# Three more weight tiles ahead of the branch, and the branch, the entry and the last two experts of each expert stage rearranged

## The chip, the cores and the metric

The kernel runs on one core of one Trainium2 chip. The metric is the device time of one execution in microseconds (us); for the kernel before it is the median of three runs. A core has five engines that run side by side, each with its own queue of instructions: TensorE (PE, matmuls), VectorE (DVE), ScalarE (ACT), GpSimd (POOL) and SyncE (SP, whose queue issues the transfers from memory here).

## The reference

Two layers over 256 tokens of width 1024. Layer 0 mixes the tokens by a convolution module, layer 1 by retention; behind each stands a mixture of 32 experts (top 2 of one group of 8). All weights are float32.

```python
for i in range(DEPTH):                      # 2 layers
    if i % 2 == 0: mix = conformer_conv(x, ...)
    else:          mix = retention(x, positions, ...)
    x = layer_norm(DEEPNORM_ALPHA * x + mix, ln1_g[i], ln1_b[i])
    ffn = hier_moe(x, ...)
    x = layer_norm(DEEPNORM_ALPHA * x + ffn, ln2_g[i], ln2_b[i])

def hier_moe(x, w_grp, b_grp, w_route, b_route, w_gate, w_up, w_down):
    ...  # combine: (256, 32), the two chosen experts' gates of each token, 0 elsewhere
    for e in range(N_EXPERTS):              # 32
        h = jax.nn.silu(xt @ w_gate[e]) * (xt @ w_up[e])     # 1024 -> 512, twice
        y = y + combine[:, e:e + 1] * (h @ w_down[e])        # 512 -> 1024
```

## The kernel before

**Stages.** Four stages follow one another: the convolution (0 to some 126 us), the experts of layer 0, the retention, the experts of layer 1. The text calls (e, q) the quarter q of the work of expert e.

**Weights.** The class `Weights` streams all weights through one queue, SP's, as pieces of 1 MiB, in the order in which they are used. An expert has six: gate and up by halves (two pieces each), down by halves (two). Each piece needs a tile: 12 ring tiles, in an expert stage two "own" ones more (pool `mp`) and two "split" ones (two half tiles each, `hi` and `lo`). `home(i)` says which kind piece i gets, `room` counts the free tiles, and `used()` gives a tile back and loads the next piece. So 16 pieces of a stage can be loaded before its first experts have used any. The pieces w12 to w27 are those of layer 0.

**The way in.** `norms` ends the stage before: for each half of the tokens (tt) it computes a layer norm, and `front(tt)` from `moe_front` transposes the result (tiles xr) and computes the router's logits (lg). Behind that, `moe` splits the activations into x1h and a remainder x1l (L898 on ScalarE, L899 on GpSimd), and `route` chooses the experts in small VectorE steps (`first_max`, L926 to L934; between them `warm` matmuls, which compute nothing that is used). TensorE counts positions (L953 to L955), and `gather` (L1011) collects up to 64 tokens for each expert by one-hot matmuls.

**An expert.** `gate_up` multiplies two 128-row slices of gate and up a quarter (L1025), `hidden` applies silu and the product, `turn` transposes h (L1045) and gathers the gates of a pair (L1049), `down` multiplies a pair of experts side by side in two column halves of the array (L1070), `places` and `parts` prepare the way back (L1080, L1090), and `scatter` adds a pair's result to the tokens (L1101). A table, `plan`, says behind which quarter of which expert each such step stands, a pair's steps one to two experts after its `gate_up`. The last pair (experts 30 and 31) stands outside the pattern: its 32 down matmuls come behind all gate and up, then `begin(1)` (L1110), then the scatter into PSUM, from which the norm at the end reads.

**The branch.** More than 64 tokens at one expert are handled by a loop in a branch (`extra`, L1126, `overflow`), which isn't entered with these inputs. All engines read the flag (L1128) and compare (L1134) at the same point of the program, between (0, 1) and (0, 2). The branch's scratch is in split tiles, and the tiles of the first two pieces are given back behind it:

```python
                if e == 0 and i == 1:
                    extra()
                    W.used(2)
                    for tt in range(2):
                        G.tensor_scalar(cur[:, tt], cur[:, tt], ALPHA, None, op0=OP.mult)
```

**Order.** `manual_schedule` keeps TensorE, ScalarE, VectorE and GpSimd in the order in which the code is written; SP's order is set by a scheduler. An instruction waits at the head of its engine's queue until what it needs is there, and all behind it wait with it.

## Time and profile before

| | us |
|---|---|
| median of three runs | 1322.53 |
| the three runs | 1321.91 to 1324.62 |
| the profiled execution | 1325.74 |
| its span | 1324.0 |
| mean granted TensorE clock | 0.977 of full |
| TensorE busy | 1264.8 (96%) |
| moved by DMA | 459.44 MB, mean 347 GB/s |

The profile is one execution, seen by the chip's profiler. The span is its time from the first to the last instruction. Busy time is time in which an engine executes; matmuls overlap one another, so the distance of two starts says more of what a matmul costs than its duration. An idle time is put down to the event that came last before the next instruction. The DMA share is the mean busy share of the core's 16 DMA engines. The clock stands as a share of full speed: 1.00 is 2.4 GHz, 0.50 is 1.2 GHz.

### The profile page before, as it was taken

How to read it: one execution, taken by the hardware profiler on the slowest of the kernel's cores; microseconds unless marked ns; L12 is line 12 of the kernel's file. 1: busy time of each engine (PE TensorE's matmuls, PEld its weight loads, DVE VectorE, ACT ScalarE, POOL GpSimd, SP SyncE). 2: the span in 40 equal slices, each digit the busy share in tenths (PEclk: the TensorE clock that was granted, in tenths of full speed). 3: DMA queues.
4: the chain of work that ended last, by engine and by line, in shares of the span. 5: the costliest groups of instructions: out<-in, count | busy, mean ns of one | idle time of the engine just before them, and what ended most of it. 6: DMA issues, size and time to landing. Idle time of an engine off the chain costs nothing. (4 is left out here: it accounts for less than half of the span.)

```text
span 1324.0 us, 15498 instructions
## 1 busy us (share of the span) xinstructions
PE 1264.8 (96%) x6139; PEld 668.2 (50%) x6139; DVE 491.0 (37%) x849; ACT 327.7 (25%) x543; POOL 164.0 (12%) x173
## 2 busy tenths in 40 slices
...
GB/s 299 399 110 185 98 387 418 426 425 425 426 425 427 425 426 425 426 426 408 247 173 202 175 193 210 100 369 419 425 425 426 425 426 426 425 425 426 425 428 125
DMA packets 102101, 459.44 MB, mean 347 GB/s; under 512 B 8226, under 2 KB 25410, under 8 KB 59010
## 3 DMA queue, kind: packets, MB, share of 16 engines
...
## 5 line engine op out<-in xcount | busy, mean ns | idle before, releaser
L1070 PE MATMUL y<-w,h 128*64 128x512 f32 x992 | 255.7, 595 | 14.8 <-DMA w<-in_moe_w_down_dram 14.8
L1025 PE MATMUL gu<-w,xghi 128*64 128x512 f32 x896 | 225.0, 612 | 0.0
L1036 DVE TENSOR_TENSOR h<-gl,gu 64x512 f32<-64x512 f32 x64 | 67.8, 1060 | 384.3 <-ACT gl L1034 372.4
L1025 PE MATMUL gu<-w,xglo 128*64 128x512 f32 x800 | 195.0, 612 | 6.6 <-PEq L1134 6.6
L1070 PEld LDWEIGHTS y<-w,h 128*64 128x64 f32 x992 | 78.1, 138 | 168.4 <-issue 143.2
L1025 PEld LDWEIGHTS gu<-w,xghi 128*64 128x64 f32 x896 | 62.4, 138 | 96.4 <-issue 88.4
L1025 PEld LDWEIGHTS gu<-w,xglo 128*64 128x64 f32 x800 | 55.8, 140 | 103.5 <-issue 97.0
L129 DVE TENSOR_TENSOR l<-w,h 128x1024 fp32r<-128x1024 f32 x64 | 81.2, 1270 | 67.9 <-ACT h L128 66.4
L1034 ACT ACTIVATE gl<-gu 64x512 f32<-64x512 f32 x64 | 37.6, 588 | 242.9 <-PE gu L1025 242.9
L128 ACT ACTIVATE h<-w 128x1024 fp32r<-128x1024 f32 x72 | 75.7, 1058 | 88.0 <-PE vg L763 31.7
L1052 ACT ACTIVATE h<-hT 128x256 f32<-128x256 f32 x64 | 24.6, 384 | 276.8 <-PE hT L1049 168.5
L1057 DVE COPY gsl<-hT 64x1 f32<-64x1 f32 x64 | 10.0, 156 | 188.1 <-ACT h L1052 187.7
L1105 DVE TENSOR_TENSOR cur<-sc,cur 128x512 f32<-128x512 f32 x116 | 72.3, 684 | 19.6 <-PE sc L1101 19.6
L129 POOL TENSOR_TENSOR l<-w,h 128x1024 fp32r<-128x1024 f32 x8 | 20.5, 2590 | 409.9 <-ACT h L128 409.9
L1090 ACT ACTIVATE yh<-y,gsl 128x512 fp32r<-128x512 f32 x64 | 44.0, 687 | 92.9 <-PE y L1070 90.5
L439 PE MATMUL pw<-xT,w 128*128 128x256 f32 x256 | 60.7, 394 | 1.8 <-DMA w<-in_conv_w_pw_dram 1.8
L472 POOL TENSOR_TENSOR gp<-gp,gt 128x256 f32<-128x256 f32 x76 | 56.2, 740 | 25.2 <-ACT gt L471 19.8
L1011 PE MATMUL gp<-oh,x1h 128*128 128x256 f32 x256 | 57.1, 304 | 2.3 <-DVE route L964 2.3
L1011 PEld LDWEIGHTS gp<-oh,x1h 128*128 128x128 f32 x256 | 38.6, 188 | 39.1 <-issue 38.1
L439 PEld LDWEIGHTS pw<-xT,w 128*128 128x128 f32 x256 | 50.3, 198 | 9.9 <-issue 2.7
L1083 DVE TENSOR_SCALAR s<-sp,cc 128x256 fp32r<-128x256 f32 x32 | 15.5, 484 | 96.3 <-PE sp L1080 96.3
L1011 PE MATMUL gp<-oh,x1l 128*128 128x256 f32 x256 | 50.8, 280 | 0.0
...
## 6 DMA issues: line engine op xcount, KB each, us to landing
w<-in_moe_w_down_dram SPq DMA_DIRECT2D x124, 1024.0 KB, 17.1
w<-in_moe_w_gate_dram SPq DMA_DIRECT2D x106, 1024.0 KB, 15.5
w<-in_moe_w_up_dram SPq DMA_DIRECT2D x106, 1024.0 KB, 16.2
w<-in_ret_w_qkvg_dram SPq DMA_DIRECT2D x24, 1024.0 KB, 13.2
...
w<-in_ret_w_o_dram SPq DMA_DIRECT2D x8, 1024.0 KB, 4.9
w<-in_conv_w_pw_dram SPq DMA_DIRECT2D x4, 1024.0 KB, 11.2
...
```

The lines of the kernel that those rows point to most:

```text
L128: self.nc.scalar.activation(hi, w, AF.Copy)
L129: (self.nc.gpsimd if pool else self.nc.vector).tensor_tensor(lo, w, hi.bitcast(F32), op=OP.subtract)
L439: PE.matmul(ps[:, 1 - g], w[g][:, kt], xT[:, kt], start=kt == 0, stop=kt == KT - 1)
L472: G.tensor_tensor(gps[c], gps[c], t, op=OP.add)
L1011: PE.matmul(ps[:, k], src[:, tt, q * 2 + k], o[:, tt].rearrange("p e c -> p (e c)"), start=i == 0, stop=i == 3)
L1025: PE.matmul(gus[e][m * CAP:(m + 1) * CAP], l, w[i % 2 * 2 + k], start=kt == 0, stop=kt == KT - 1)
L1034: S.activation(gl, gu[:CAP], AF.Silu)
L1036: V.tensor_tensor(hs[e].rearrange("s k p -> s p k"), gl.rearrange("s (p k) -> s p k", k=4), gu[CAP:].rearrange("s (p k) -> s p k", k=4), o ...
L1052: S.activation(hs[e], p, AF.Copy)
L1070: PE.matmul(ys[pr][n][j * CAP:(j + 1) * CAP], hs[e][:, kt], wds[e][kt % 2][:, n * 512:(n + 1) * 512], start=kt == 0, stop=kt == 3)
L1090: S.activation(yh[:, n], ys[pr][n], AF.Copy, scale=g)
L1105: V.tensor_tensor(o, ps, o, op=OP.add)
```

## The change

- **Tiles.** `ONCE` names three pieces of a stage (numbers 7, 16 and 17) that get tiles of their own, once: one a pair of split half tiles, two others four half tiles of the pool `hand`, which the transposed rows xr leave (`more`, called behind the norm). With them 19 pieces (w12 to w30) come before the branch, and the sequence of the other homes skips them.
- **Branch.** It stands behind (0, 3) instead of (0, 1); its scratch is in two ring tiles (`spare`). The scaling of `cur` behind it goes from GpSimd to ScalarE.
- **Entry.** The norm of the stage before is now called inside `moe`. The split x1h, x1l is done by quarters: ScalarE copies half the tokens in `front(tt)` (`high`), GpSimd takes one quarter of the remainder, VectorE three (`low`). `WARM` has two values less by one, and the last `first_max` has no warm matmuls at its end.
- **Last two experts.** Each goes alone: its down matmuls put the two halves of the output in the two column halves, its scatter uses 64 rows a half. Expert 30's first down steps move ahead of the end of expert 31's gate and up, `begin(1)` ahead of them, and the splits of the next stage's weights (`ahead`) stand among them: two by VectorE, two by GpSimd, where GpSimd had all four.
- The rotary tables are built at experts 3 and 10 instead of 0 and 4.

```diff
 RING = 12
+ONCE = {7: "split", 16: "hand", 17: "hand"}
 T4 = 9
 SPLIT = 4
-AH = 2
 ROWS_AT = (29, 0)
-WARM = [11, 8, 8, 0, 2, 0, 2, 3]
+WARM = [11, 8, 8, 0, 2, 0, 1, 2]
 YB = 2
...
     def home(self, i):
         for a, b in self.layers:
             if a <= i < b:
-                return ("ring", "own", "split")[max(0, (i - a) % (RING + 4) - RING + 2) // 2]
-        return "ring"
+                k = i - a
+                if k in ONCE:
+                    return "once", ONCE[k]
+                k -= sum(x < k for x in ONCE)
+                return ("ring", "own", "split")[max(0, k % (RING + 4) - RING + 2) // 2], None
+        return "ring", None
 
     def open(self, pool):
 
         self.own = pool
-        self.room.update(own=2, split=2)
-        self.load(4)
+        self.room.update(own=2, split=2, once=1)
+        self.load(6)
+
+    def more(self):
+
+        self.room["once"] = len(ONCE) - 1
+        self.load(2)
...
+    def spare(self, name):
+
+        t = self.ringp.tile([P, 2048], F32, tag="ring", name=name, bufs=RING)
+        return t[:, 0:1024], t[:, 1024:2048]
...
-    for p in range(NE // 2):
+
+    for p in range(NE // 2 - 1):
         e, both = 2 * p + 2, (2 * p, 2 * p + 1)
         planned(e - 1, 0, ("turn", e - 2))
-        if p < NE // 2 - 1:
-            planned(e, 0, ("turn", e - 1))
-            planned(e, 2, ("down", both, 0))
-            planned(e, 3, ("down", both, 1))
-            planned(e + 1, 0, ("down", both, 2))
-            planned(e + 1, 1, ("down", both, 3), ("parts", p))
+        planned(e, 0, ("turn", e - 1))
+        planned(e, 2, ("down", both, 0))
+        planned(e, 3, ("down", both, 1))
+        planned(e + 1, 0, ("down", both, 2))
+        planned(e + 1, 1, ("down", both, 3), ("parts", p), *([("place", -2)] if p == NE // 2 - 2 else []))
+        if p < NE // 2 - 2:
             planned(e + 2, 0, ("scatter", p))
-        else:
-            planned(e, 0, ("turn", e - 1), *[("down", both, k) for k in range(4)])
-    planned(NE - 2, 3, ("begin", 0))
+    z = NE - 1
+    planned(z - 1, 3, ("begin", 0))
+    planned(z, 0, ("turn", z - 1))
+    planned(z, 2, ("down", (z - 1,), 0), ("scatter", NE // 2 - 2), ("down", (z - 1,), 1), ("place", -1))
+    planned(z, 3, ("begin", 1), ("down", (z - 1,), 2), ("down", (z - 1,), 3), ("part", -2), ("turn", z),
+            *[("down", (z,), k) for k in range(4)], ("ahead", 2), ("part", -1), ("ahead", 4), ("scatter", -2),
+            ("scatter", -1))
...
+        def view(t, tt, n):
+            return t[:, tt, :, n * 64:(n + 1) * 64].rearrange("t k p -> t p k")
+
+        def row(tt, n):
+            return cur[:, tt, n * 512:(n + 1) * 512].rearrange("t (p k) -> t p k", k=KT)
+
+        def high(tt):
+            for n in range(2):
+                S.activation(view(x1h, tt, n), row(tt, n), AF.Copy)
+
+        def low(tt, n, eng=V):
+            eng.tensor_tensor(view(x1l, tt, n), row(tt, n), view(x1h, tt, n).bitcast(F32), op=OP.subtract)
+
         def front(tt):
             if tt == 0:
                 xT.extend(hand(f"xr{L}{q}", F32) for q in range(2))
                 mark["lg"] = sm1("lg")[:, 0:72].rearrange("p (a b) -> p a b", a=2)
+            else:
+                low(0, 1)
             lgp = mark["lg"]
             PE.matmul(lgp[:, tt], onesf[0:1, :], brt[0:1, L], start=True, stop=False, skip_group_check=True)
             transposes(tt, evac)
+            high(tt)
             ts = slice(tt * P, (tt + 1) * P)
             for kt in range(KT):
                 PE.matmul(lgp[:, tt], xT[kt // 4][:, kt % 4, ts], wrt[:, L, kt], start=False, stop=kt == KT - 1,
                           skip_group_check=True)
+            if not tt:
+                low(0, 0, G)
+            else:
+                low(1, 0)
+                mark["low"] = lambda: low(1, 1)
...
             W.open(mp)
             with tc.tile_pool(name=f"exp{L}", bufs=1) as ep:
-                for tt in range(2):
-                    v = cur[:, tt].rearrange("t (p k) -> t p k", k=KT)
-                    hv = x1h[:, tt].rearrange("t k p -> t p k")
-                    lv = x1l[:, tt].rearrange("t k p -> t p k")
-                    S.activation(hv, v, AF.Copy)
-                    G.tensor_tensor(lv, v, hv.bitcast(F32), op=OP.subtract)
-                route(L, ep, lgp, comb, posm, posT, flag)
+                norms(*prev, moe_front(L, x1h, x1l))
+                W.more()
+                route(L, ep, mark["lg"], comb, posm, posT, flag)
...
-            warm(WARM[7], f)
+            if not last:
+                warm(WARM[7], f)
...
-        m2, oh2 = first_max(me, 32)
+        m2, oh2 = first_max(me, 32, last=True)
...
+        mark["low"]()
...
+            single = e >= NE - 2
+            if single:
+                for j in range(2):
+                    for tt in range(2):
+                        PE.matmul(ps[j * CAP:(j + 1) * CAP, 256:257], ohs[e // 4][:, tt, e % 4].bitcast(F32),
+                                  comb[:, tt, e:e + 1], start=tt == 0, stop=tt == 1)
...
-                    j = e % 2
-                    PE.matmul(ys[pr][n][j * CAP:(j + 1) * CAP], hs[e][:, kt], wds[e][kt % 2][:, n * 512:(n + 1) * 512],
+                    j, b = (e % 2, n) if len(es) > 1 else (n, 0)
+                    PE.matmul(ys[pr][b][j * CAP:(j + 1) * CAP], hs[e][:, kt], wds[e][kt % 2][:, n * 512:(n + 1) * 512],
                               start=kt == 0, stop=kt == 3)
...
+                    ks = slice(0, P) if pr >= 0 else slice(n * CAP, (n + 1) * CAP)
                     for i in range(2):
-                        PE.matmul(ps, s0[pr][:, tt * P:(tt + 1) * P], ys[pr][i][:, n], start=not held and i == 0,
-                                  stop=i == 1 and (pr == NE // 2 - 1 or not held))
+                        PE.matmul(ps, s0[pr][ks, tt * P:(tt + 1) * P], ys[pr][i][ks, n if pr >= 0 else 0],
+                                  start=not held and i == 0, stop=i == 1 and (pr == -1 or not held))
...
+                elif what == "ahead":
+                    W.stop = len(pieces)
+                    W.ahead(*step, pool=step[0] > 2)
...
-            wts, big = [splitp.tile([P, 1024], F32, tag=t, name=f"ov{t}{L}") for t in ("hi", "lo")]
-            mid = [ep.tile([P, 512], F32, tag="gl", name="ovgl")[:CAP]]
-            mid += [hand(n, F32).rearrange("p a t -> p (a t)")[:CAP] for n in ("ovh", "ovy")]
+            (wts, big), mid = [W.spare(f"ov{n}{L}") for n in range(2)]
+            mid = [ep.tile([P, 512], F32, tag="gl", name="ovgl")[:CAP], *[m[:CAP] for m in mid]]
...
-                if e == 0 and i == 1:
+                if e == 0 and i == 3:
                     extra()
                     W.used(2)
                     for tt in range(2):
-                        G.tensor_scalar(cur[:, tt], cur[:, tt], ALPHA, None, op0=OP.mult)
+                        S.activation(cur[:, tt], cur[:, tt], AF.Copy, scale=ALPHA)
...
-            if L == 0 and e == 0:
+            if L == 0 and e == 3:
                 mark["rot"] = rotary_tables()
-            if L == 0 and e == 4:
+            if L == 0 and e == 10:
                 mark["rot"]()
-        p = NE // 2 - 1
-        places(p)
-        run(NE, 0)
-        begin(1)
-        parts(p)
-        W.stop = len(pieces)
-        W.ahead(AH, pool=True)
-        scatter(p, fin)
```

**SP's queue up to the branch of layer 0.** The names w12 to w30 are the pieces of layer 0's experts; a name with hi, lo, 0 or 1 behind the number is half a piece. Before:

```order
L112 DMA w23_1054<-in_moe_w_up_dram 128x2048
L96 DMA w26lo_1197<-in_moe_w_gate_dram 128x1024
L96 DMA w26hi_1195<-in_moe_w_gate_dram 128x1024
L96 DMA w27hi_1199<-in_moe_w_up_dram 128x1024
L112 DMA w24_1191<-in_moe_w_down_dram 128x2048
L112 DMA w25_1193<-in_moe_w_down_dram 128x2048
L96 DMA w27lo_1201<-in_moe_w_up_dram 128x1024
L1128 TENSOR_LOAD flag_1190
L1128 ISA x2
```

After:

```order
L123 DMA w26_1207<-in_moe_w_gate_dram 128x2048
L107 DMA w280_1330<-in_moe_w_down_dram 128x1024
L107 DMA w281_1332<-in_moe_w_down_dram 128x1024
L107 DMA w290_1716<-in_moe_w_down_dram 128x1024
L107 DMA w291_1718<-in_moe_w_down_dram 128x1024
L107 DMA w270_1326<-in_moe_w_up_dram 128x1024
L107 DMA w300_1720<-in_moe_w_gate_dram 128x1024
L107 DMA w271_1328<-in_moe_w_up_dram 128x1024
L107 DMA w301_1722<-in_moe_w_gate_dram 128x1024
L1187 TENSOR_LOAD flag_1103
L1187 ISA x2
L1192 COMPARE_AND_BRANCH
```

Behind w26 four halves that didn't stand ahead of the flag (w28, w29) and one more piece (w30) come before the flag's load.

**ScalarE in the norm ahead of layer 0's experts.** lnc0sd and lnc1sd are the square roots of the two halves' variances, xr the transposed rows. Before:

```order
L315 ACTIVATE lnc0sd_1111<-lnc0mv_1109,epsc_149 128x1
L867 ACTIVATE xr00_1119<-tr00_1123 128x4x128
L867 ACTIVATE xr01_1120<-tr01_1129 128x4x128
L315 ACTIVATE lnc1sd_1148<-lnc1mv_1146,epsc_149 128x1
L867 ACTIVATE xr00_1119<-tr10_1161 128x4x128
L898 ACTIVATE x1h_1185<-cur_75 128x128x8 x2
```

After:

```order
L338 ACTIVATE lnc0sd_1128<-lnc0mv_1126,epsc_149 128x1
L890 ACTIVATE xr00_1136<-tr00_1140 128x4x128
L890 ACTIVATE xr01_1137<-tr01_1146 128x4x128
L900 ACTIVATE x1h_1098<-cur_75 128x64x8 x2
L338 ACTIVATE lnc1sd_1168<-lnc1mv_1166,epsc_149 128x1
L890 ACTIVATE xr00_1136<-tr10_1182 128x4x128
L900 ACTIVATE x1h_1098<-cur_75 128x64x8 x2
```

The copies to x1h of the first half of the tokens moved ahead of the second half's square root.

**TensorE at the end of layer 1's experts.** sc and fin are the targets of the scatter, hT transposes h, y is the down product (y15 the last pair's, y-2 and y-1 those of the experts 30 and 31). Before:

```order
L1101 MATMUL fin01_8789<-yh14_8826,s014_8824 128x512
L1101 MATMUL fin01_8789<-yl14_8827,s014_8824 128x512
L1101 MATMUL sc1410_8853<-yh14_8826,s014_8824 128x512
L1101 MATMUL sc1410_8853<-yl14_8827,s014_8824 128x512
L1101 MATMUL sc1411_8857<-yh14_8826,s014_8824 128x512
L1101 MATMUL sc1411_8857<-yl14_8827,s014_8824 128x512
L1045 MATMUL hT31_8861<-ident_140,h31_8842 128x64 x4
L1070 MATMUL y150_8868<-w424_8699,h3230_8808 64x512
...
L1070 MATMUL y151_8869<-w426lo_8724,h3230_8808 64x512
L1070 MATMUL y151_8869<-w427lo_8728,h3231_8866 64x512
L1110 MATMUL fin10_8886<-cur_75,ident_140 128x512
L1110 MATMUL fin11_8887<-cur_75,ident_140 128x512
L1101 MATMUL fin00_8788<-yh15_8890,s015_8847 128x512
```

After (the places and the last four gate and up matmuls stand at the dots):

```order
L1153 MATMUL sc1411_8863<-yh14_8837,s014_8835 128x512
L1153 MATMUL sc1411_8863<-yl14_8838,s014_8835 128x512
L1121 MATMUL y-20_8852<-w424_8713,h3230_8820 64x512 x2
...
L1162 MATMUL fin10_8882<-cur_75,ident_140 128x512
L1162 MATMUL fin11_8883<-cur_75,ident_140 128x512
L1121 MATMUL y-20_8852<-w425_8734,h3230_8820 64x512 x4
L1086 MATMUL hT31_8894<-ident_140,h31_8880 128x64 x4
L1091 MATMUL hT31_8894<-comb_5894,oh7_8362 64x1 x4
L1121 MATMUL y-10_8907<-w426_8736,h3231_8903 64x512 x4
L1121 MATMUL y-10_8907<-w427_8774,h3231_8903 64x512 x4
L1153 MATMUL fin00_8798<-yh-2_8890,s0-2_8846 128x512
L1153 MATMUL fin00_8798<-yl-2_8891,s0-2_8846 128x512
```

The down product of expert 30 starts behind the scatter of pair 14 and is split by gate and up and by begin (fin10, fin11); each of the two experts has its own gates (L1091), and a scatter of its own follows.

## Rows read from the trace of the kernel before

**Rows 1.** from the page, parts 1, 2 and 6: busy time, share of the span and instructions of each engine; what the DMA engines moved in each of 40 equal slices of 33.1 us (GB/s); one kind of DMA issue with its KB and median us from issue to landing.
```profile
PE 1264.8 (96%) x6139; PEld 668.2 (50%) x6139; DVE 491.0 (37%) x849; ACT 327.7 (25%) x543; POOL 164.0 (12%) x173
...
GB/s 299 399 110 185 98 387 418 426 425 425 426 425 427 425 426 425 426 426 408 247 173 202 175 193 210 100 369 419 425 425 426 425 426 426 425 425 426 425 428 125
...
w<-in_moe_w_gate_dram SPq DMA_DIRECT2D x106, 1024.0 KB, 15.5
```

**Rows 2.** what TensorE waited for: line, releaser, us in total, times, longest.
```profile
PE y L1070 <- DMA w<-in_moe_w_down_dram: 14.8, 18, 1.4
PE gu L1025 <- PEq L1134: 6.6, 2, 3.3
...
PE sc L1101 <- DVE s L1083: 1.0, 2, 0.5
```

**Rows 3.** layer 0, one stretch of 10 us in which TensorE waits for weights: width, busy us of each engine with instructions, granted TensorE clock (PEclk), DMA share, GB/s.
```profile
430.00:440.00 10.00, 8.36 (x34) 2.64 (x30) 1.07 (x1) 0.59 (x1) 0.00 (x0) 1.00 1.02 422
```

**Rows 4.** DMA issues on SP's queue around the first branch, in order of time.
```profile
126.53 0.42 SPq L96 DMA_DIRECT2D w27lo<-in_moe_w_up_dram  x1
157.79 1.47 SPq L112 DMA_DIRECT2D w<-in_moe_w_down_dram  x2
```

**Rows 5.** stretches of 1 us: layer 0, columns as in Rows 3.
```profile
137.00:138.00 1.00, 1.00 (x4) 0.30 (x4) 1.00 (x1) 0.00 (x0) 1.00 (x1) 0.50 0.00 0
157.00:158.00 1.00, 0.90 (x3) 0.34 (x5) 0.00 (x0) 0.00 (x0) 1.00 (x1) 0.50 0.10 25
161.00:162.00 1.00, 1.00 (x8) 0.36 (x6) 0.00 (x0) 0.00 (x0) 0.00 (x0) 1.00 1.00 418
```

**Rows 6.** TensorE from the gather of the first experts to behind the first branch, in order of time: start, us, line, operation, and the idle time before with its releaser.
```profile
145.60 0.47 PE L1011 MATMUL gp<-oh,x1h 128*128 128x256 f32 x2 [1.14 <-DVE route L964]
...
151.82 1.94 PE L1025 MATMUL gu<-w,xghi 128*64 128x512 f32 x8
157.10 5.26 PE L1025 MATMUL gu<-w,xglo 128*64 128x512 f32 x16 [3.35 <-PEq L1134]
```

**Rows 7.** the two lines of the branch, one after the other, TensorE's queue alone: duration min/median/max in ns, first and last start.
```profile
L1134 PEldq COMPARE_BRANCH  x2: 3402/3436/3470, 153.4 to 852.9; - x2
...
L1128 PEldq EVENT_SEMAPHORE  x8: 51/51/1839, 150.7 to 852.4; - x8
```

**Rows 8.** the way into layer 0's experts, all engines, in order of time.
```profile
126.57 1.08 ACT L867 ACTIVATE xr<-tr 128x512 f32<-128x512 f32 x2 [5.25 <-PE tr L342]
...
127.54 0.29 ACT L315 ACTIVATE lnc1sd<-lnc1mv,epsc 128x1 f32<-128x1 f32 x1
...
128.59 1.40 DVE L329 SCALAR_TENSOR_TENSOR cur<-cur,r,ln1b 128x512 f32<-128x512 f32 x2
...
131.29 3.74 ACT L898 ACTIVATE x1h<-cur 128x1024 fp32r<-128x1024 f32 x2
...
133.40 5.66 POOL L899 TENSOR_TENSOR x1l<-cur,x1h 128x1024 fp32r<-128x1024 f32 x2 [26.03 <-DMA w<-in_moe_w_down_dram]
...
133.92 2.36 DVE L930 SCALAR_TENSOR_TENSOR route<-route,cc 128x8 f32<-128x8 f32 x1
...
136.51 2.58 DVE L934 TENSOR_TENSOR route<-route 128x8 f32<-128x8 f32 x1
...
139.89 0.23 DVE L930 SCALAR_TENSOR_TENSOR route<-route,cc 128x64 f32<-128x64 f32 x1
...
143.59 0.81 PE L276 MATMUL warm<-onesb 128*128 128x512 bf16 x3
...
144.24 0.18 PE L953 MATMUL pos<-route,triub 128*128 128x32 bf16 x1
```

**Rows 9.** the chain that ended last, the end of layer 1's experts: start, us, what.
```profile
1290.57 0.54 PE hT L1049 x4
...
1294.69 0.23 PE sp L1080 x2
1294.91 3.61 PE gu L1025 x16
...
1301.94 7.55 PE y L1070 x32
1309.49 1.91 PE fin L1110 x4
...
1311.92 1.30 DVE lnm10st L311 x2
```

**Rows 10.** TensorE at the same end, in order of time: the starts of two matmuls in two column halves, and of two scatter matmuls.
```profile
1268.12 0.64 PE L1025 MATMUL gu<-w410hi,xglo 128*64 128x512 f32 x1
1268.13 0.64 PE L1025 MATMUL gu<-w411hi,xglo 128*64 128x512 f32 x1
...
1299.22 0.40 PE L1101 MATMUL fin<-yh,s 128*128 128x512 f32 x1
1299.46 0.40 PE L1101 MATMUL fin<-yl,s 128*128 128x512 f32 x1
```

**Rows 11.** the norm at the end of layer 0, all engines, in order of time.
```profile
614.73 10.24 POOL L129 TENSOR_TENSOR l<-w,h 128x1024 fp32r<-128x1024 f32 x4 [409.85 <-ACT h L128]
...
618.35 4.39 DVE L329 SCALAR_TENSOR_TENSOR cur<-cur,r,rows 128x512 f32<-128x512 f32 x2
...
622.80 1.12 PE L342 MATMUL tr<-ident,cur 128*128 128x128 f32 x4 [2.10 <-DVE cur L329]
```

73 lines of the change are left out of this document (41 added, 32 removed).

## The prediction

> **What bounds the kernel now.** The page comes first. TensorE is busy 96% of the span, and in both expert stages the DMA engines move 425 to 427 GB/s, slice after slice [rows 1]. Two resources are full at once, so the list of what TensorE waits for decides: 14.8 us on weights in 18 waits, 7.4 us a layer [rows 2]. Where they stand, around 430 us, TensorE is busy 8.36 of 10 us, the DMA share is 1.02 and the clock is full [rows 3]: there the loads set the time, elsewhere the matmuls do, by little. So a layer's experts end with the last weights, and what counts first is when the loads begin, how many are left then, and only then what TensorE does.
>
> They begin late. SP issues its last piece before the branch at 126.53 us and the next at 157.79 [rows 4]; the DMA engines stand still in between, as the stretch from 137 to 138 shows [rows 5]. One MiB at 426 GB/s is 2.46 us. What holds SP is a chain: routing, gather, two quarters of the first expert, the branch. After its last matmul before the branch TensorE idles 3.35 us in layer 0, 6.6 us in both [rows 2, 6], beside a COMPARE_BRANCH of 3.40 to 3.47 us on its queue [rows 7].
>
> **The change, part by part.** I follow one layer's loads from the norm to the last weight; all terms are us earlier (+) or later (-).
>
> *Three more tiles, +7.4.* 19 instead of 16 pieces are in before the branch: 3 x 2.46 = 7.4. There is room for them: the still stretch is some 22 us long, and the four half tiles that come last wait for the buffers of the transposed rows, which the logits read last, just before VectorE's routing steps at 133.92 [rows 8], and 2.0 later now (below): free at about 135.5, on the chip by about 146, beside the gather. If that cover were gone, each would cost its 2.46 again.
>
> *The way in, +3.2.* The difference x - x1h leaves GpSimd, but for a quarter. Beside GpSimd's 5.66 us two VectorE instructions took 2.36 and 2.58; one of them, repeated alone on eight times the elements, takes 0.23. That is +4.5. Against it, ScalarE's copy of the first half of the tokens (3.74 for two halves, so 1.87) now stands ahead of the second norm's square root, which ran at 127.54 inside the copies of the transposed rows, which end at 127.65; it will now start at about 129.5: -2.0. The final warm matmuls, which kept TensorE until the position matmuls at 144.24, lose two of three: +0.7, an estimate from the 0.81 that three of them took just ahead of it. Sum 3.2 [rows 8]. Bounds: 4.5 if ScalarE's copy finds cover, 1.0 if half the VectorE stall stays beside the quarter that GpSimd keeps (1.4 us of 5.66) and the 0.7 is not there. VectorE's own three quarters wait for ScalarE and stand where VectorE waits for the logits, at nothing; uncovered they would cost about 0.7 each, half of the 1.40 of two such passes.
>
> The trace has shown VectorE blocked beside GpSimd [rows 8]; the Trainium skill, "SBUF — State Buffer", section "Who interferes with whom", gives the rule: a VectorE instruction with two SBUF inputs contends with a GpSimd instruction that reads SBUF. The trace agrees for 2.36 against 0.23. The rule speaks against the quarter left on GpSimd and, at layer 0's end, against the two differences left there. By it, where each of them meets a VectorE instruction, a layer's way in would be 1.4 worth less and the norm nothing: 2 x 1.4 + 1.6 = 4.4 on top of the sum below, 1311.9; by the rows alone the sum stands.
>
> *The branch two quarters later, -1.5.* From the first gather matmul at 145.60 to SP's issue at 157.79 are 12.19 us [rows 4, 6]. Now two more quarters of gate and up stand before it, 16 matmuls: 3.61 at full clock [rows 9] (after the branch they took 5.26 [rows 6], at half clock at first [rows 5]). For that the branch may hide: TensorE's queue stood at the flag from 150.7 and waited 1.84 us [rows 7], while its matmuls ran to about 153.76 (151.82 + 1.94 [rows 6]). The flag comes when the turned matmuls are done, which hasn't moved, so with 3.61 us more of matmuls queued the queue reaches the compare with 2 to 4 us of work in hand; I take 2.1 of 3.4 as hidden. Bounds: all 3.4 (-0.2) and none (-3.6). Behind the waiting branch on SP stand the pieces for the ring's last two tiles, since the branch's scratch is in them, and all others behind these; who waits for them is TensorE, some 19 pieces later.
>
> *Loads together:* 7.4 + 3.2 - 1.5 = 9.1 earlier; bounds 7.4 + 1.0 - 3.6 = 4.8 and 7.4 + 4.5 - 0.2 = 11.7. TensorE must follow. Without its waits for weights it could come 7.4 + 3.2 + 2.1 = 12.7 earlier, so the loads stay last and about 3.6 of the 7.4 us of waits remain.
>
> *The end of a layer, -2.4.* The last pair becomes two single experts, so that half of the last down work is done before the last gate and up. The 32 matmuls of 7.55 [rows 9] keep their number and their pairing in column halves. Added on TensorE: 8 more scatter matmuls at 0.24, the distance of two starts [rows 10], 1.9; one more place, 0.23; gate matmuls for one expert each instead of one pair, 8 instructions for 2 of 0.54 together [rows 9], smaller ones, for which I take 0.8 (bounds 0.5 and 1.6). Removed: the 0.5 wait for s [rows 2]. Net 2.4; bounds 0.9, if half the scatters overlap others, and 3.5, if the wait stays and the gates are dear. The 1.91 of begin(1), which in the kernel before covers the parts' way through ScalarE and VectorE [rows 9], stands earlier now; the first single's 8 scatters take over as cover, 1.9 for 1.9. The last weights are needed at the same point of the order, and land earlier, so the gain of 9.1 is not stopped here.
>
> *Layer 0's norm, +1.6, once.* There VectorE's two scalings took 4.39 instead of 1.40 [rows 8, 11], beside four differences on GpSimd, 10.24 long, and TensorE waited 2.10 for them [rows 11]. Now two of the four go to VectorE, and GpSimd's two start later: I take 1.6, bounds 0 and 2.1.
>
> *At nothing:* scaling cur on ScalarE instead of GpSimd, since ScalarE is busy 25% [rows 1]; the rotary tables, moved from expert 0 to 3, used a stage later; the retention stage, which is not fed any later.
>
> **The sum.** 9.1 - 2.4 = 6.7 a layer, 13.4 for two, and 1.6: 15.0 us. The profiled execution took 1325.74 us, so 1310.7; it lies 3.2 over the median of 1322.53, and in the median's terms I forecast **1307.5**. Bounds of all terms: 2 x (4.8 - 3.5) = 2.6 and 2 x (11.7 - 0.9) + 2.1 = 23.7 us, that is 1319.9 and 1298.8.
>
> **Rivals.** *R1, the queue isn't ahead at the branch.* For it: the waits for the flag are of a queue that has run dry before; TensorE idled after the compare in both layers [rows 2]. Then the 3.4 stay and the loads come 7.4 + 3.2 - 3.6 = 7.0 earlier; if the two quarters before the branch run for some 3 us at the lower clock too, as from 157 to 158 (0.50, full at 161 [rows 5]), 1.6 more is lost. A layer gains 5.4 - 2.4 = 3.0, both and the norm 7.6: **1314.9**.
>
> *R2, the end costs next to nothing.* The scatters of a single expert contract over 64 rows, one half of the array. Column halves start 0.01 apart [rows 10]; if row halves of two neighbours did so too, 16 half scatters would take the time of 8, and with 0.5 left of the rest a layer gains 9.1 - 0.5: 18.8, **1303.7**. The trace shows no row halves; the neighbours write the same bank, which speaks against it.
> The Trainium skill, "TensorEngine Tiling (Array Packing)", section "Key Properties", says that different tiles of the array can load and multiply in parallel; for column halves the trace agrees, for row halves it shows nothing.
>
> *R3, slower: the loads now hang on the clock.* The granted clock was 0.50 in the stretch at 137 and again at 157, after TensorE had idled [rows 5]. Fewer warm matmuls leave TensorE idle more often before the gather. If it stays at 1.2 GHz from the gather to the end of the first expert, its 8.2 us of work before the branch and the 3.6 that the change puts there take twice as long: 11.8 later, before all loads. A layer then gains 9.1 - 11.8 - 2.4 = -5.1, and with 1.6 the kernel takes 8.6 more, **1331**. It decides from a restart that is 7.5 us later than I reckon ((2 x 6.7 + 1.6) / 2). Against it: with warm matmuls cut only at the end, the gather follows within 2 us; and before, the 8 matmuls at 151.82 took 1.94 [rows 6], the pace of the 16 in 3.61 at the kernel's end [rows 9], so the clock had recovered.
>
> *R4, the change doesn't bring its loads.* If the tiles come free only behind the routing, the three pieces are read in the busy time after all; 7.4 falls away, with the end's 2.4 against the way in and the branch (3.2 - 1.5) a layer loses 0.7 and the norm gives 1.6: **1322.3**.
>
> **How the numbers follow.** My forecast has 0.53, R1 0.17, R2 0.14, R3 0.09, R4 0.07. The forecast's own spread is about 5 us each way (its branch and way-in bounds, not all at once), so from 1303 to 1313. The range should leave out R3, half of R4 and the ends of the rest: 1299.5 to 1318. Within 0.2% of the time before, 2.6 us, is about what a measurement of this kernel can tell from no change. Faster by more: forecast, R1 and R2 but for their tails, 0.82. Same: R4 and those tails, 0.08. Slower: R3 and a hundredth of others, 0.10.
>
> **What would show it.** In layer 0 SP issues the last half tiles at about 136 and the next piece at about 156 (157.79 - 3.2 + 1.5); DMA waits fall from 14.8 to about 7; the first L930 and L934 take some 0.2 each; TensorE's idle time behind the compare is 1 to 1.5, not 3.35. The way from the last expert's first quarter to the norm is 2.4 longer. The forecast is wrong if SP restarts after 158, if the clock is 0.50 in the gather, or if waits for weights stay near 14.8 although SP restarts in time: then loads were never what is last.

## The result, and the profile after

The changed kernel takes 1301.48 us in the median of four runs (1297.08 to 1306.94), beside 1323.34 of before (four runs, 1321.91 to 1324.62): ratio 0.9836, 95% interval 0.9803 to 0.9870, so some 22 us faster. The forecast was 1307.5 with a range from 1299.5 to 1318, that is 15.0 faster. A second measurement of the same kernel (e1 below) gave the ratio 0.9834 (0.9819 to 0.9849). The profiled execution is the slowest of the four, 1306.94 with a span of 1305.2, 18.8 below the span before.

The page, busy time and GB/s in 40 slices (of 32.6 us), to compare with [rows 1]:

```profile
PE 1257.0 (96%) x6163; PEld 667.3 (51%) x6163; DVE 487.9 (37%) x859; ACT 334.1 (26%) x553; POOL 139.3 (11%) x165
...
GB/s 317 391 110 177 194 421 425 426 425 426 425 426 426 426 426 426 425 426 407 225 196 179 175 207 200 224 412 413 425 425 426 425 428 425 425 425 425 425 423 48
```

Both expert stages still move 425 GB/s; their first slices are fuller (421 for 387, 412 for 369), and the last slice of the kernel has 48 instead of 125. What TensorE waits for, as in [rows 2]:

```profile
PE y L1121 <- DMA w<-in_moe_w_down_dram: 11.1, 12, 1.7
...
PE hT L1086 <- DVE h L1077: 1.8, 2, 1.0
...
PE gu L1066 <- DMA w<-in_moe_w_up_dram: 1.1, 2, 0.6
...
PE gu L1066 <- PEq L1192: 0.8, 2, 0.5
```

The wait behind the compare fell from 6.6 to 0.8. The waits for weights fell from 14.8 to 12.2 (11.1 + 1.1), not to the 7 of the forecast. SP's queue around the first branch (start, us, issue), as in [rows 4]:

```profile
129.05 6.23 SPq L107 DMA_DIRECT2D w<-in_moe_w_down_dram  x4
...
136.75 1.90 SPq L107 DMA_DIRECT2D w<-in_moe_w_gate_dram  x1
156.21 0.34 SPq L123 DMA_DIRECT2D w<-in_moe_w_up_dram  x1
```

The half tiles go out from 129 to 137, and the first piece behind the branch at 156.21: forecast 136 and 156. That the second agrees is partly luck. Layer 0's norm came 1.4 us earlier here than in the profile before (its statistics at 124.98 instead of 126.38); that isn't the change's doing, for in the experiments' profiles they lie between 123.1 and 126.5. Counted from the statistics, SP restarts at 31.2 instead of 31.4, and in layer 1 at 29.6 instead of 30.9: 0.2 and 1.3 earlier, where 1.7 was forecast. The branch's line, TensorE's queue alone, as in [rows 7]:

```profile
L1192 PEldq COMPARE_BRANCH  x2: 3579/3740/3902, 152.2 to 838.9; - x2
```

The compare is no shorter, 3.58 to 3.90 us; it lies under queued matmuls now. The way in, all engines, in order of time, as in [rows 6, 8]:

```profile
127.91 0.27 ACT L338 ACTIVATE lnc1sd<-lnc1mv,epsc 128x1 f32<-128x1 f32 x1
...
135.36 0.17 DVE L969 SCALAR_TENSOR_TENSOR route<-route,cc 128x8 f32<-128x8 f32 x1
...
135.76 0.17 DVE L974 TENSOR_TENSOR route<-route 128x8 f32<-128x8 f32 x1
...
141.43 0.76 PE L1052 MATMUL gp<-oh,x1h 128*128 128x256 f32 x2 [1.55 <-DVE route L1005]
...
145.11 2.97 PE L1066 MATMUL gu<-w,xghi 128*64 128x512 f32 x8
...
150.32 1.94 PE L1066 MATMUL gu<-w,xghi 128*64 128x512 f32 x8
...
152.09 3.60 PE L1066 MATMUL gu<-w,xglo 128*64 128x512 f32 x16
...
156.23 1.94 PE L1066 MATMUL gu<-w,xghi 128*64 128x512 f32 x8 [0.54 <-PEq L1192]
```

The two VectorE steps take 0.17 instead of 2.36 and 2.58; ScalarE's square root ran at 127.91, where 129.5 was expected; counted from the statistics it came 1.8 later than before, close to the 2.0 of the forecast. TensorE gathers at 141.43 instead of 145.60, but then takes 2.97 for the first 8 gate and up matmuls instead of 1.94, and idles 0.54 instead of 3.35 at the branch. Why the 2.97, the stretches of 2 us there show (width, busy us of each engine with instructions, clock, DMA share, GB/s):

```profile
128.00:130.00 2.00, 0.95 (x6) 0.49 (x5) 1.79 (x4) 0.18 (x2) 0.90 (x1) 1.00 1.00 422
130.00:132.00 2.00, 2.00 (x12) 1.64 (x11) 1.70 (x3) 1.35 (x2) 0.00 (x0) 0.54 0.98 365
...
144.00:146.00 2.00, 2.00 (x8) 1.18 (x9) 0.00 (x0) 0.76 (x2) 0.00 (x0) 0.50 0.62 244
...
148.00:150.00 2.00, 2.00 (x18) 1.94 (x16) 0.00 (x0) 0.60 (x1) 0.00 (x0) 1.00 0.00 0
```

The granted clock fell to 0.50 as the norm's last part began and came back only at 147; TensorE was busy for 0.95 of 2 us just before it fell. In the kernel before it was 0.50 for less long, from 137 [rows 5] to 143. The end of layer 1, TensorE in order of time, as in [rows 9, 10]:

```profile
1287.45 3.65 PE L1121 MATMUL y-10_8907<-w,h 128*64 128x512 f32 x16 [0.49 <-ACT h L1099]
1291.03 0.50 PE L1153 MATMUL fin<-yh-2_8890,s0-2_8846 64*128 64x512 f32 x2
1291.37 0.40 PE L1153 MATMUL fin<-yl-2_8891,s0-2_8846 64*128 64x512 f32 x2
1291.60 0.40 PE L1153 MATMUL fin<-yh-2_8890,s0-2_8846 64*128 64x512 f32 x2
1291.84 0.39 PE L1153 MATMUL fin<-yl-2_8891,s0-2_8846 64*128 64x512 f32 x2
1292.07 0.39 PE L1153 MATMUL fin<-yh-1_8916,s0-1_8872 64*128 64x512 f32 x1
1292.68 0.50 PE L1153 MATMUL fin<-yl-1_8917,s0-1_8872 64*128 64x512 f32 x1 [0.22 <-DVE yl-1_8917 L1142]
```

The scatters of single experts use 64 rows of the array ("64*128"), and two of them, one for each half, start together: the first eight take 1.04 (from 1291.03 to 1292.07), not 1.9. The scalings in layer 0's norm, as in [rows 11]:

```profile
606.78 2.56 DVE L352 SCALAR_TENSOR_TENSOR cur<-cur,r,rows 128x512 f32<-128x512 f32 x2
```

2.56 instead of 4.39. From the first of the norm's statistics to TensorE's first matmul of the retention (v, L683 before, L706 now) it is 6.8 us instead of 8.2. And one stretch of layer 1, in steps of 2 us, in which TensorE waits for weights:

```profile
1228.00:1230.00 2.00, 0.50 (x2) 0.00 (x0) 0.00 (x0) 0.00 (x0) 0.00 (x0) 1.00 1.01 422
1230.00:1232.00 2.00, 1.07 (x2) 0.19 (x2) 0.00 (x0) 0.00 (x0) 0.00 (x0) 1.00 1.01 426
...
1234.00:1236.00 2.00, 2.00 (x4) 0.23 (x1) 0.00 (x0) 0.00 (x0) 0.00 (x0) 0.50 1.00 422
...
1240.00:1242.00 2.00, 2.00 (x10) 1.80 (x9) 0.00 (x0) 0.60 (x1) 0.00 (x0) 0.50 1.01 420
...
1248.00:1250.00 2.00, 2.00 (x12) 0.72 (x12) 1.80 (x3) 0.56 (x1) 0.00 (x0) 1.00 1.00 422
```

TensorE is busy 0.50 and 1.07 of 2 us, and behind that the clock is low twice, from 1233 to 1236 and from 1239 to 1246: for 10 us TensorE then works at half pace. Whether that lengthens the stage is what e8 asks.

**One table for all that follows.** Each experiment left one profiled execution. From the row of the norm's statistics (BATCH_NORM_AGGREGATE of lnc1mv in layer 0, lnr1mv in layer 1) to three points, us, layer 0 / layer 1: SP's first issue behind the gather; the transposes of expert 1's h, where TensorE has the branch behind it; and those of expert 30, where most waits for weights lie behind it. The stage's length to the last point is free of what the conv and the retention took in that execution. The last column is what the DMA engines moved from 30 us ahead of the statistics to 100 us behind them (GB/s; 8.07 of these are one MiB).

| | SP's issue | expert 1 | expert 30 | two stages | moved by 100 us |
|---|---|---|---|---|---|
| before | 31.4 / 30.9 | 48.9 / 48.8 | 467.2 / 464.1 | 931.2 | 263 / 274 |
| changed | 31.2 / 29.6 | 42.1 / 40.7 | 455.6 / 456.9 | 912.5 | 297 / 312 |
| e1, changed again | 29.8 / 30.8 | 41.8 / 42.0 | 456.3 / 455.1 | 911.5 | 298 / 309 |
| e2, no more tiles | 25.6 / 26.0 | 42.1 / 40.7 | 461.0 / 459.6 | 920.6 | 278 / 293 |
| e3, branch early | 31.7 / 29.6 | 47.8 / 45.7 | 459.1 / 460.2 | 919.4 | 278 / 297 |
| e9, neither | 31.5 / 30.8 | 47.2 / 46.9 | 465.4 / 462.7 | 928.0 | 269 / 280 |
| e5, old entry | 30.9 / 30.9 | 41.8 / 41.6 | 453.8 / 453.5 | 907.3 | 297 / 310 |
| e6, old warm matmuls | 31.0 / 30.1 | 41.8 / 41.0 | 455.7 / 455.3 | 910.9 | 298 / 310 |
| e12, no branch | 25.3 / 27.3 | 41.6 / 43.6 | 456.3 / 456.2 | 912.5 | 296 / 303 |

These are single executions. e5 lies 4 us below e1 with as much moved and expert 1 as early, so differences of a few us in the fourth column decide nothing by themselves. The last column's lines for layer 0 of e1, e3 and e12, each from its own profile:

```profile
93.18:223.18 130.00, 123.39 (x591) 66.30 (x592) 50.64 (x112) 40.73 (x67) 32.61 (x41) 0.93 0.77 298
93.13:223.13 130.00, 119.39 (x559) 65.41 (x559) 48.03 (x108) 39.74 (x65) 27.58 (x34) 0.91 0.73 278
94.88:224.88 130.00, 123.30 (x593) 66.46 (x594) 51.01 (x118) 39.35 (x66) 32.66 (x41) 0.93 0.79 296
```

### The profile page after: what moved, and what is told of

Same layout as the page of the kernel before. It is cut to its first block, busy times and chain, and to the rows that moved or that the text cites. A ratio compares the mean times of both kernels' runs of the same rounds, so it can differ in the third digit from the quotient of the medians.

```text
span 1305.2 us, 15536 instructions
## 1 busy us (share of the span) xinstructions
PE 1257.0 (96%) x6163; PEld 667.3 (51%) x6163; DVE 487.9 (37%) x859; ACT 334.1 (26%) x553; POOL 139.3 (11%) x165
## 4 chain that ended last, share of the span: by engine, by line
PE 55%; DMA 30%; DVE 2%; ACT 1%; issue 0%; DVEq 0%; SPq 0%; ACTq 0%
PE gu L1066 20%; DMA w<-in_moe_w_up_dram 14%; DMA w<-in_moe_w_down_dram 13%; PE y L1121 9%; PE gp L1052 3%; PE sc L1153 3%; DMA w<-in_moe_w_gate_dram 2%; PE vg L784 2%; PE vg L785 2%; PE vg L786 2%; PE qk L767 1%; PE qk L766 1%; PE qk L764 1%; PE hT L1086 1%; PE wo L652 1%; PE wo L653 1%
## 5 line engine op out<-in xcount | busy, mean ns | idle before, releaser
L1066 PE MATMUL gu<-w,xghi 128*64 128x512 f32 x1024 | 254.4, 611 | 1.9 <-DMA w<-in_moe_w_up_dram 1.1
L1121 PE MATMUL y<-w,h 128*64 128x512 f32 x960 | 242.6, 598 | 11.1 <-DMA w<-in_moe_w_down_dram 11.1
L1066 PE MATMUL gu<-w,xglo 128*64 128x512 f32 x1024 | 242.1, 598 | 0.0
L1121 PEld LDWEIGHTS y<-w,h 128*64 128x64 f32 x960 | 73.3, 138 | 158.5 <-issue 137.1
L1066 PEld LDWEIGHTS gu<-w,xglo 128*64 128x64 f32 x1024 | 69.8, 136 | 118.4 <-issue 109.3
L1066 PEld LDWEIGHTS gu<-w,xghi 128*64 128x64 f32 x1024 | 68.7, 138 | 111.9 <-issue 101.0
L139 ACT ACTIVATE h<-w 128x1024 fp32r<-128x1024 f32 x72 | 75.7, 1058 | 88.0 <-PE vg L786 31.7
L1141 ACT ACTIVATE yh<-y,gsl 128x512 fp32r<-128x512 f32 x60 | 41.2, 687 | 79.9 <-PE y L1121 79.8
L140 POOL TENSOR_TENSOR l<-w,h 128x1024 fp32r<-128x1024 f32 x6 | 14.9, 2518 | 369.4 <-ACT h L139 369.4
## 6 DMA issues: line engine op xcount, KB each, us to landing
w<-in_moe_w_up_dram SPq DMA_DIRECT2D x116, 1024.0 KB, 14.8
w<-in_moe_w_gate_dram SPq DMA_DIRECT2D x106, 1024.0 KB, 14.7
w<-in_moe_w_gate_dram SPq DMA_DIRECT2D x44, 512.0 KB, 14.7
```

The source lines that it names most:

```text
L139: self.nc.scalar.activation(hi, w, AF.Copy)
L140: (self.nc.gpsimd if pool else self.nc.vector).tensor_tensor(lo, w, hi.bitcast(F32), op=OP.subtract)
L1066: PE.matmul(gus[e][m * CAP:(m + 1) * CAP], l, w[i % 2 * 2 + k], start=kt == 0, stop=kt == KT - 1)
L1121: PE.matmul(ys[pr][b][j * CAP:(j + 1) * CAP], hs[e][:, kt], wds[e][kt % 2][:, n * 512:(n + 1) * 512], start=kt == 0, stop=kt == 3)
L1141: S.activation(yh[:, n], ys[pr][n], AF.Copy, scale=g)
```

## The experiments

All are edits of the changed kernel, each timed beside the kernel before on the same chip, whose median lay between 1324.0 and 1326.9. Ratios are to before; one thousandth is 1.3 us.

**e1, the changed kernel again.**

> The changed kernel once more, unaltered, as the measure for the three others of this chip. Both theories: 1301.5 us, within 3, about 21 faster than before. If the low clock ahead of the first gather (0.50 in the profiled execution, 140 to 146 us) is what spreads its runs, a profiled execution with a higher clock there lies lower, by up to some 3.5 us a layer.

1302.72 (1301.97 to 1303.80), ratio 0.9834 (0.9819 to 0.9849): as expected.

**e2, without the three tiles.**

```diff
-ONCE = {7: "split", 16: "hand", 17: "hand"}
+ONCE = {}
```

> ONCE is empty: 16 pieces come before the branch instead of 19, all else as changed. Theory L (loads set the end of an expert stage): three pieces, 7.4 us a layer, fall into the busy time, the waits for weights grow by that, and the kernel takes 14.8 more than the changed one: about 1316. Theory T (TensorE's own path sets it; the tiles are mostly hidden): TensorE's waits for weights grow by no more than 2 a layer, about 1305.

1314.7, ratio 0.9919 (0.9899 to 0.9939): 0.0085 or 11 us slower than changed, nearer to 14.8 than to 3. TensorE waits 15.6 for weights in its profile. In the table the tiles are worth 9.1 for two stages. By 100 us behind the statistics the loads are 36 GB/s, or 4.5 MiB, behind e1 in two stages, not 6: part of the three pieces is made up for in the stretch in which the loads aren't full. So the tiles count, with some 60 to 75% of their 14.8.

**e3, the branch early.**

```diff
-                if (e, i) != (0, 3):
+                if (e, i) != (0, 1):
...
-                if e == 0 and i == 3:
+                if e == 0 and i == 1:
                     extra()
```

> The branch is moved back behind the second quarter, with its scratch in ring tiles and with the 19 pieces. Theory L: the loads start again some 0.7 earlier after the gather (3.6 less work ahead of it, 2.9 of the branch uncovered), but two tiles are free then instead of four, and the first 30 us of loads run at some 376 instead of 412 GB/s as in the kernel before, 2.9 worse: 2.2 a layer, about 1306. Theory T: TensorE loses the 2.9 of idle time behind the compare in each layer, about 1307, and its waits for weights shrink by as much. That the branch's place is worth nothing: 1301.5.

1311.64, ratio 0.9902 (0.9886 to 0.9918): 0.0068 or 9 us slower, about twice what either theory gave. TensorE around the branch of layer 0:

```profile
148.57 1.94 PE L1066 MATMUL gu<-w,xghi 128*64 128x512 f32 x8
154.36 3.65 PE L1066 MATMUL gu<-w,xglo 128*64 128x512 f32 x16 [3.86 <-ACT cur L1210]
...
162.03 3.05 PE L1066 MATMUL gu<-w,xghi 128*64 128x512 f32 x8
```

Its last matmul before the branch ends at 150.51, and it idles 3.86 until 154.36 (the profile names ScalarE's scaling, the event that came last; the compare on TensorE's own queue took 3.84). And the 8 matmuls at 162.03 take 3.05 instead of 1.94. The same kernel by stretches:

```profile
164.00:166.00 2.00, 2.00 (x8) 0.73 (x6) 0.00 (x0) 0.00 (x0) 0.00 (x0) 0.50 1.00 418
170.00:180.00 10.00, 9.91 (x56) 4.85 (x52) 0.85 (x1) 1.58 (x3) 0.00 (x0) 1.00 0.92 353
180.00:190.00 10.00, 10.00 (x54) 4.31 (x55) 1.14 (x2) 2.17 (x4) 0.00 (x0) 1.00 0.80 306
```

The clock was 0.50 there, from 163 to 166, as in the kernel before behind its branch [rows 5]; the changed kernel's profile shows 1.00 from 148 to 180. So one early branch costs some 3 of idle time (3.86 and 3.11 in the two layers, where the changed kernel has 0.54 and 0.25) and 1.7 of clock (3.4 us at half clock in either layer), and TensorE reaches expert 1 6.0 and 3.7 later than in e1 (47.8 / 45.7 for 41.8 / 42.0). The part of the clock isn't as sure as that of the idle time: behind the branch the clock fell in all six stages with the early branch that were profiled (before, e3, e9), but also in three of twenty with the late one, layer 0 of e1 among them (157 to 160). The loads follow it: 353 and 306 GB/s from 170 to 190, where e1 has 381 and 418, although SP's first issue comes about where the changed kernel's two profiles have it.

**e4, the last two experts as a pair,** with `plan`, `begin(1)` and the four differences on GpSimd as in the kernel before:

```diff
-    for p in range(NE // 2 - 1):
+    for p in range(NE // 2):
...
-            single = e >= NE - 2
+            single = False
...
+        p = NE // 2 - 1
+        places(p)
+        run(NE, 0)
+        begin(1)
+        parts(p)
+        W.stop = len(pieces)
+        W.ahead(2, pool=True)
+        scatter(p, fin)
```

> The last two experts go as a pair again, with begin and the four differences on GpSimd as in the kernel before; entry, tiles and branch as changed. By the prediction's term the single experts cost 2.4 a layer and the norm behind layer 0 gains 1.6: 1298.3. By the trace (the half-array scatters start in pairs; from the last gate and up's first quarter to the norm 26.8 instead of 25.3 us) they cost 0.7 to 1.5 a layer, and the norm gains 0.8: 1300. If expert 30's early down work is worth something to the loads, it gets slower: over 1303.

1300.62, ratio 0.9813 (0.9796 to 0.9830), 0.0021 below the changed kernel with intervals that overlap: the single experts show no gain, and cost at most a few us. In the profiles, from the last gate and up's first quarter to layer 1's norm, it takes 25.4 as before, and 26.9 in the changed kernel: 1.5 more a layer.

**e5, the old entry:** no `high` and `low` in the norm; behind it, as before:

```diff
+                for tt in range(2):
...
+                    S.activation(hv, v, AF.Copy)
+                    G.tensor_tensor(lv, v, hv.bitcast(F32), op=OP.subtract)
                 W.more()
```

> The split into x1h and x1l goes back behind the norm, whole halves on ScalarE and GpSimd as before; tiles, branch, end and warm matmuls as changed. Theory L (the loads set the end, so the way to the gather counts): the gather comes some 2.5 later after the norm in each layer (18.5 to 19 instead of 14.7 to 16.6), 5 to 6 in all, about 1308. Theory T (TensorE's own path sets it and the loads ride along): the same, since the path to the first gate and up is later too; the rival is that the waits for weights behind it take the difference up: 1303.

1304.88, ratio 0.9842 (0.9811 to 0.9873): 0.0008 or 1 us slower, the rival's; the intervals overlap, so none can't be told from it, while the 5 to 6 of the theories lie at their edge. VectorE's two steps took 2.23 and 2.57 again in layer 0. The gather came 17.5 behind the statistics in both layers, 0.9 to 2.8 later than in the changed kernel's two profiles, and expert 1 was reached at the same 41.8 and 41.6: from the gather to SP's next issue it took 13.4, where the changed kernel took 13.9 to 15.1. Most of what VectorE had gained on the way in, the clock took back: it was 0.50 as the gather began in both kernels, but for 3.0 and 2.8 us more in e5 and for 4.5 to 5.8 in the four stages of the changed kernel's two profiles.

**e6, the old warm matmuls.**

```diff
-WARM = [11, 8, 8, 0, 2, 0, 1, 2]
+WARM = [11, 8, 8, 0, 2, 0, 2, 3]
...
-        m2, oh2 = first_max(me, 32, last=True)
+        m2, oh2 = first_max(me, 32)
```

> All warm matmuls of the routing as before, all else as changed. Theory C (the low clock of the way in comes from TensorE's idle stretches, and the warm matmuls shorten them): the granted clock ahead of the gather is 1.00 for longer, the gather and the two first quarters take some 2 less a layer, and 0.7 of warm matmuls stands against it: about 1300. Rival (as the prediction has it): the clock is 0.50 there either way, as in the kernel before, and the warm matmuls cost 0.7 a layer: 1304.

1298.76 (1292.72 to 1303.67), ratio 0.9783 (0.9747 to 0.9819). Its profiled execution in stretches of 2 us:

```profile
134.00:136.00 2.00, 2.00 (x9) 1.08 (x9) 1.76 (x10) 0.21 (x1) 0.00 (x0) 0.50 0.65 203
140.00:142.00 2.00, 0.87 (x8) 0.46 (x6) 1.08 (x4) 0.00 (x0) 0.00 (x0) 1.00 1.02 412
```

The clock is back at 1.00 by 140, where the changed kernel's two profiles have it at 143 and 147. The gather comes 18.8 and 18.2 behind the statistics, later than in e1 (14.7 and 16.6), and from there to SP's next issue it takes 12.2 and 12.0 instead of 15.1 and 14.3: an even exchange, and the table shows 41.8 and 41.0 to expert 1. So the mechanism of theory C is there, and its gain isn't in this execution. The 5 us of the median are those of other executions, with more clock overall (1292.72 at a mean of 0.986, the profiled one 1302.27 at 0.977); where they gained it wasn't profiled.

**e7, all four differences on GpSimd.**

```diff
-                    W.ahead(*step, pool=step[0] > 2)
+                    W.ahead(*step, pool=True)
```

> All four differences for the next stage's weights go to GpSimd again, at the changed place; it concerns layer 0's norm alone. The prediction's term: 1.6 later, 1304.3. By the trace of the changed kernel (VectorE's scalings 2.56 for two instead of 4.39): 1.8 later, 1304.5. Rival: the differences start earlier now than in the kernel before, so GpSimd is done before the scalings begin and nothing changes: 1302.7.

1303.96, ratio 0.9830 (0.9798 to 0.9861): no difference, as the rival has it. GpSimd's four differences start at 598.88 and take 9.34, so only the last lies beside the scalings, which start at 606.65 and take 2.77 (2.56 in the changed kernel, beside the last difference too). The gain in that norm came from the earlier start; it doesn't need the second engine.

**e8, filled waits.**

```diff
+FILL = {(10, 0): 5, (12, 2): 3, (13, 0): 5}
...
             if kt % 2 == 0:
+                if len(es) > 1:
+                    warm(FILL.get((pr, kt), 0))
```

> The changed kernel with 5, 3 and 5 warm matmuls (some 0.22 each at full clock) ahead of the down work of the pairs 10, 12 and 13 at the steps where TensorE waits for weights. Theory C: the waits are idle stretches behind which the clock was granted 0.50 (551 to 557 and 1233 to 1246 in the profiled execution of the changed kernel, some 3 and 5 us of work lost); filled, the clock stays at 1.00 there, the matmuls themselves lie in waits: about 1297, and the runs spread less. Rival: the loads are last there anyway, so what the clock loses the waits give back, and the filling adds up to 1.3 at each place that doesn't wait: 1303 to 1308.

1302.08, ratio 0.9817 (0.9785 to 0.9849), 0.0017 below the changed kernel: inconclusive. The stretches of 4 us behind the waits of both layers:

```profile
550.00:554.00 4.00, 4.00 (x19) 3.16 (x19) 0.00 (x0) 1.79 (x3) 0.00 (x0) 0.52 1.03 425
1231.00:1235.00 4.00, 3.18 (x17) 1.71 (x18) 0.00 (x0) 0.29 (x1) 0.00 (x0) 1.00 1.00 424
1235.00:1239.00 4.00, 4.00 (x35) 3.59 (x36) 0.31 (x2) 2.41 (x5) 0.00 (x0) 1.00 1.00 416
```

In layer 1 the clock stayed at 1.00, where the changed kernel had 0.71 and 0.86 in the same two stretches; in layer 0 it fell to 0.52 all the same. Expert 30 was reached 451.0 behind the statistics in layer 1 (456.9 and 455.1 in the changed kernel's two profiles) and 455.8 in layer 0 (455.6 and 456.3): that fits theory C, in one execution.

**e9, neither tiles nor late branch:** the edits of e2 and e3 together.

> ONCE empty and the branch behind the second quarter: of the change only the entry, the end, the norm and the warm matmuls are left. Theory A (tiles and branch add up, one earns in the loads, the other in TensorE's idle time and in the clock behind it): 12.0 and 8.9 more than the changed kernel, ratio to before 0.9834 + 0.0085 + 0.0068 = 0.999. Rival O (they overlap, as without the tiles the loads are last and TensorE's idle time at the branch costs nothing): 12 to 14 more, ratio 0.993.

1317.85, ratio 0.9947 (0.9931 to 0.9963), between the two theories: 15 us slower than changed, where the sum is 20 and the overlap 12 to 14. In the table they do add up: 928.0 - 911.5 = 16.5, of 9.1 (e2) and 7.9 (e3). So tiles and branch make 15 of some 22 us by the medians and 16.5 of 19.7 (931.2 - 911.5) by the table. What is left of the change makes e9 itself 0.0053 or 7 us faster than before; it reaches expert 1 1.7 and 1.9 earlier than the kernel before.

**e10 and e11, pair and old warm matmuls together, without and with filled waits:** the edits of e4 and e6, then that of e8.

> The last two experts as a pair and all warm matmuls of the routing, both as before, all else as changed. If the two add up (-0.0021 and -0.0051 of the ratio): 0.976, about 1292 where before is 1323.5. If the gain of the old warm matmuls was chance (its profiled execution reaches its first loads behind the branch no earlier than the changed kernel's: 31.0 and 30.1 us behind the norm's statistics, 31.2 and 29.6 there): 0.981, 1299.

1301.89, ratio 0.9836 (0.9816 to 0.9856): what e4 and e6 had gained did not come again together.

> The same with the filled waits (5, 3 and 5 warm matmuls at pairs 10, 12, 13). In the profiled execution with filled waits the second layer's clock stayed at 1.00 behind them and the first layer's didn't, 1.5 gained and 1.3 lost. Theory C: 0.5 to 2 us below the kernel without them. Rival: no difference that can be told, within 2.

1299.27 (1293.06 to 1306.61), ratio 0.9794 (0.9769 to 0.9819). That is 0.0042 below e10, at the edge of both intervals; with e8's 0.0017 the filling may be a gain, but no version is shown to beat the changed kernel clearly. Its profiled execution is the slowest of the six (1306.61), with the clock at 0.50 from 1230 to 1247 in spite of the filling.

**e12, no branch at all.**

```diff
-            rv = nc.values_load(flag[0:1, 0:1], min_val=0, max_val=T * NE)
...
-            with tc.If(rv > 0):
-                overflow(L, x1h, x1l, comb, posm, wts, big, mid, row, pair)
+            for t in (wts, big, mid[0], row, pair[0], pair[1]):
+                V.memset(t[:1, 0:1], 0.0)
```

> The changed kernel without the branch: the flag's read, the compare and the loop for experts with more than 64 tokens are left out (with these inputs the loop isn't entered); its scratch tiles stay and get one small VectorE write each. It shows what the branch still costs. Theory W (what counts is how soon tiles come back and loads follow): the loads go on as the first two tiles come free, some 150 instead of 153 to 156, and TensorE saves the 0.2 to 0.5 behind the compare: 1 to 3 a layer, 1297 to 1301. Rival G (the gate at the branch holds all loads of a layer back by the whole stretch from the third half tile's landing on, some 6 us): 6 a layer, 1290. Rival N (nothing is left to win there): 1302.7.

1304.95, ratio 0.9853 (0.9829 to 0.9878): the time is rival N's, no gain. SP's queue (start, us, issue):

```profile
135.15 0.65 SPq L107 DMA_DIRECT2D w<-in_moe_w_gate_dram  x1
150.18 0.33 SPq L123 DMA_DIRECT2D w<-in_moe_w_up_dram  x1
...
153.57 0.33 SPq L123 DMA_DIRECT2D w<-in_moe_w_up_dram  x1
...
160.42 0.33 SPq L123 DMA_DIRECT2D w<-in_moe_w_up_dram  x1
```

SP goes on at 150.18, 25.3 behind the statistics instead of 29.8 (e1). The same kernel by stretches:

```profile
150.00:160.00 10.00, 8.61 (x42) 3.18 (x40) 2.18 (x10) 2.78 (x4) 0.00 (x0) 0.92 0.90 351
160.00:170.00 10.00, 9.91 (x47) 3.75 (x44) 1.06 (x1) 1.57 (x3) 0.00 (x0) 0.90 0.99 366
170.00:180.00 10.00, 10.00 (x54) 4.68 (x55) 1.06 (x1) 1.78 (x3) 0.00 (x0) 1.00 0.77 255
200.00:210.00 10.00, 10.00 (x52) 3.74 (x50) 1.07 (x1) 0.90 (x2) 9.09 (x12) 1.00 1.01 427
```

But the loads then run at 351, 366 and 255 GB/s for 30 us, and at 427 only from some 200 on. What SP's own queue waited for from 145 to 215, in the changed kernel and in e12 (us in total, times, longest):

```profile
SPq L123 <- PE gu L1066: 38.2, 8, 6.9
SPq L123 <- PE gu L1066: 57.6, 10, 14.3
```

Each piece waits for a tile that TensorE gives back: by the fifth piece behind the gather SP is hardly further than with the branch (35.5 and 37.4 behind the statistics, 36.0 and 36.7 in e1), and the earlier restart is lost in that. TensorE didn't reach expert 1 earlier without the branch either (41.6 and 43.6): the clock was 0.50 for 3.4 us in both layers, from 158 and from 848. What e12 would gain with the full clock there, it doesn't show.

## Why the prediction was right, and which terms were off

Right were the direction, the range and part of the mechanism: 19 pieces are in before the branch (so not R4); the compare is hidden, not shortened (so not R1); the two VectorE stalls are gone. The sum was 15.0, the measured change some 22 in the medians and 18.8 in the spans. That the time lies in the range is partly luck: over both layers the branch was worth 11 to 12 us more than forecast, the tiles and the way in together 9 to 12 less, and the step beneath these terms was wrong. One of the prediction's own signs of being wrong came true as well, the clock of 0.50 in the gather.

**The step that failed** is "So a layer's experts end with the last weights, and what counts first is when the loads begin ... and only then what TensorE does", with "TensorE must follow". For the first 40 to 50 us behind the branch it doesn't matter first when SP goes on, but how soon tiles come back, that is how far TensorE is. In e12 SP is free 4 us earlier, waits for tiles, and the stage is no shorter (456.3 / 456.2). In e3 SP goes on about as early as in the changed kernel, TensorE is 4 to 6 us later, and in layer 0 the loads run at 306 to 402 GB/s from 160 to 200. (In layer 0 of the changed kernel's first profile the restart and the tiles nearly meet: from 160 to 200 the loads run at 385 to 428.) From about 200 on they are full in all these runs, and the table's last column then tells the stage's length, at 0.305 us a GB/s (2.46 us a MiB): against e1 the two stages of e2 are 36 short, 11.0 us, and 9.1 longer; of e3 32, 9.8 and 7.9; of e9 58, 17.7 and 16.5; of the kernel before 70, 21.4 and 19.7; of e12 8, 2.4 and 1.0. So each layer's end hangs on TensorE's lead up to there plus the tiles that were loaded ahead.

**The branch, -1.5 forecast.** By that step a later branch only delays loads. In fact it brings TensorE to expert 1 some 5 us earlier (e3 against e1: 6.0 and 3.7): 3 of idle time and 1.7 of clock behind it. Undone, the table loses 7.9 for two layers, so the term is +3.9 each; the median says 9 for two. I had 2.1 hidden from TensorE's side (it was 2.8 and 3.0), and put that into no gain.

**The tiles, +7.4 forecast.** e2: 9.1 for two stages in the table, 11 in the median, 4.6 to 5.6 each. The term took all three pieces for won; by 100 us 2.2 of them are still ahead. TensorE's waits for weights shrank less than reckoned (12.2 left, not 7; 15.8 without the tiles). That TensorE itself came earlier and met the loads again would explain it, but no run shows it alone.

**The way in, +3.2 forecast.** In the profile the gather is 2.8 and 3.4 earlier behind the statistics (16.5 and 15.8 for 19.2), so up to the gather the size was right. But the split's part is worth 0 to 1 us in all (e5). Rival R3 named what took it: the clock was 0.50 as the gather began in all four expert stages that the two profiles of the changed kernel show, for 4.5 to 5.8 us more. R3's size, 11.8 a layer, was far too large, since the clock came back during the first quarter or ahead of it. The prediction's reason against it, the warm matmuls cut only at the end, was wrong. The clock fell during the norm already, as the stretch from 130 to 132 shows, and the warm matmuls decide whether it is back in time: with all of them it was 1.00 as the gather began in all eight profiled stages (before, e6, e10, e11), with the fewer ones 0.50 in 18 of 20. They make the gather later, though, which in e6 took up what the clock gave.

That two steps of VectorE were held up by GpSimd is shown by e5 too, where they took 2.23 and 2.57 again. The Trainium skill's rule for them ("SBUF — State Buffer", "Who interferes with whom") holds in this trace, 0.17 against 2.36.

**The end, -2.4 forecast.** It costs 1.5 a layer in the profile, and e4 puts both layers at 0 to 3. R2's mechanism is there in part: the half-array scatters of two halves start together, eight in 1.04, and the next eight, of which one waits, in some 1.7. The Trainium skill's sentence that different tiles of the array can load and multiply in parallel ("TensorEngine Tiling (Array Packing)", "Key Properties") agrees with the trace for row halves too. R2's time, 1303.7, is nearer than the forecast, but the difference lies in the branch. Of what the end still costs the trace shows 0.49 in which TensorE waits for h of the last expert (1287.45), 0.22 for the last scatter's input (1292.68), and one more place.

**The norm, +1.6 forecast.** The scalings take 1.8 less, and TensorE goes on 1.4 sooner behind the statistics (6.8 for 8.2), so the size was right. Its reason was only half of it: in e7, with all four differences on GpSimd again, it is 7.0, since their earlier start does nearly the same.

Measured, the parts for both layers are then: tiles 9 to 11, branch 8 to 9, the split on the way in 0 to 1, end -3 to 0, norm 1.4 in the profile. Open stays what makes up the rest, 3 us by the table and up to 7 by the medians (e9 against before): the way in was never undone as a whole, split and warm matmuls together, nor was the scaling of cur on ScalarE. Open is also whether the warm matmuls of the routing are worth anything: e6 and e10 contradict each other.
